# Hybrid RWKV-7 and attention block: decay taken onto the keys, group norm and rates moved along the tile

## The chip, the core and the metric

The kernel runs on one core of a Trainium2 chip. The metric is the device time of one execution in microseconds; times given for a kernel are medians of several runs on the chip. The core's engines run apart from each other and are tied by semaphores: PE (TensorE, matmuls), DVE (VectorE), ACT (ScalarE), POOL (GpSimd) and SP (SyncE, which issues most of the DMAs). Each engine takes its instructions strictly in the order in which they were issued to it.

## What is computed

One encoder block on 512 tokens of width 2048: an input projection with 86 strips of 128 columns, a bidirectional RWKV-7 branch (16 heads of 64, two directions), a grouped-query attention branch, two branch projections merged by gates, an output projection, a residual and a final norm. The part that the change touches is the RWKV recurrence and the group norm behind it:

```python
def _wkv_step(S, inp):
    w, kk, b, k, v, r = inp
    sa = jnp.einsum('dbhvk,dbhk->dbhv', S, -kk)
    S = S * w[..., None, :] + sa[..., None] * b[..., None, :] + v[..., :, None] * k[..., None, :]
    o = jnp.einsum('dbhvk,dbhk->dbhv', S, r)
    return S, o
...
    wkv = outs[0] + jnp.flip(outs[1], axis=1)
    mu = jnp.mean(wkv, axis=-1, keepdims=True)
    var = jnp.mean(jnp.square(wkv - mu), axis=-1, keepdims=True)
    gn = (wkv - mu) * lax.rsqrt(var + GN_EPS)
    gn = gn * _heads(gn_w.astype(f32)) + _heads(gn_b.astype(f32))
    coef = jnp.sum(rh[None] * k_eff * _heads(r_k.astype(f32)), axis=-1, keepdims=True).sum(0)
    out = gn + coef * vh
```

## The kernel before

The recurrence is done in chunks of 64 tokens (`NC` = 8 of them), for eight tiles of two heads each, counted here from 0 to 7. A tile passes through these steps:

- `stage_a` (L481 on), the **rates**: a 1 MB load of `la`, then `la` is mapped (L504), the sums of squares `pss` (L498) are normalised over POOL (L261) and DVE (L503) and brought back by the transposes `prb` (L508); decays are summed by a scan for each direction (L517), turned round (L522), and ACT takes exponentials (L530 to L532). POOL and DVE multiply them into the scaled keys `BK` (L538), two halves of 128 rows for each of two directions and two sources, eight instructions in all, and into `PC`, the decay of a whole chunk (L533).
- `tile_task` first forms `AL` (L556, L559), then the **chunk-local products** `lr` (L571), two chunks at a time, in four pairs with dense matmuls between them. Each pair fills two PSUM tiles; they are masked out of PSUM by four DVE instructions (L574, L575, L577, L578) and copied by two on ACT (L573, L576). All `lr` tiles come from one pool of three buffers, tag `g`.
- the **inverse**: 32x32 triangular systems, solved on DVE by 30 steps of two instructions each (L607, L608) between transposes (L592, L595, L611, L616); it ends with copies into `XX` (L622, L625). Meanwhile PE transposes `BK` (`tb`, L633).
- two small products `pq` and `px` (L645, L653), whose results ACT copies to `LQ` (L649) and `XP` (L657), complete the inverse.
- the **chain**: for each of eight chunks PE does `pa` (L678), `pu` (L693) and `px2` (L700, shown by the trace as px of L700), ACT copies between them, and DVE forms the next state `SV` (L706) from `px2` and `sd`, the old state times `PC`, which POOL has made (L689).
- `stage_e`, the **group norm** (L722 to L730 on DVE, with a POOL power at L261), then transposes `pg` (L736), ACT copies, two DVE instructions with weights, bias and gate (L742, L743), and a store by POOL.

Beside these stand the **dense matmuls** `acc` (L291), three of 128x512 for each of 16 row blocks of a strip; their weights come by SP, and each block of 12 matmuls needs one ACT cast `wh` (L264) and one DVE difference `wl` (L265). PE's order is written out by a planner, `Weave`: tasks yield a cost and a delay in planned ns, and while no task is due it puts a dense matmul, each counted with `UNIT` = 217 ns. So a delay of a task is a number of dense matmuls: `subwait` = 50000 between the last `tb` and `pq`, `c1`, `c2`, `c3` inside the chain, 2300 between pairs of `lr`. What the RWKV part does not use of the dense matmuls fills the attention part behind it. The orders on DVE, ACT, POOL and SP are set by the tile framework's scheduler, not by hand.

Of the kernel before, what the change touches and what calls it, by code (L numbers as in the profile page):

```python
# [8 lines left out]
F32 = mybir.dt.float32  # L9
F32R = mybir.dt.float32r  # L10
AF = mybir.ActivationFunctionType
ALU = mybir.AluOpType
AX = mybir.AxisListType
# [3 lines left out]
T = 512  # L17
D = 2048
NKT = 16
C = 64  # L20
NC = T // C
NT = 8
# [78 lines left out]
class Weave:  # L101
# [3 lines left out]

    UNIT = 217
    LAG = 100
# [105 lines left out]

OPT = dict(manual=True, tls=True, sub="dve", subwait=50000, fwait=6000, gn=15000, u1=0, u2=0, c1=700, c2=700, c3=1150, fly=3, scale='pool', prb=4, low=1300, warm=24, rwt='tile', every=2, auto=1, man=1)

# [9 lines left out]
def emit_all(nc, tc, A, out, dbg):  # L225
    ve, ac, po, pe, sp = nc.vector, nc.scalar, nc.gpsimd, nc.tensor, nc.sync
# [4 lines left out]
    def tap(name, ap):  # L231
        if dbg is not None and name in dbg:
            sp.dma_start(out=dbg[name], in_=ap)
# [79 lines left out]
    def temp(nm, dt=F32):  # L313
        return rw.tile([128, T], dt, name=nm, tag="e", bufs=4)
# [105 lines left out]
    def g_tile(nm):  # L420
        return pr_.tile([128, T], F32, tag="g", name=nm, bufs=3)
# [56 lines left out]

    fact = {}

    def stage_a(i):  # L481
# [21 lines left out]
        ve.tensor_copy(rb, rs[:, 8:16].rearrange("p (t h) -> p t h", h=2).unsqueeze(3).to_broadcast([128, 4, 2, C]))  # L503
        ve.tensor_scalar(out=la, in0=la, scalar1=0.5, scalar2=0.5, op0=ALU.mult, op1=ALU.add)  # L504
        yield 250, 4500, None
        prb = g_tile("prb")
        for tt in range(4):
            pe.transpose(prb[:, tt * 128:(tt + 1) * 128], rb[:, tt].rearrange("p h c -> p (h c)"), ident)  # L508
        ve.tensor_tensor(out=kk, in0=kk, in1=prb, op=ALU.mult)
        ks = rw.tile([128, T], F32, name="ks", bufs=2)  # L510
        dirs = []
# [31 lines left out]
        W.flag(f"A{i}", 6000)  # L543
        yield 428, 0, None

    def tile_task(i):
# [16 lines left out]
        for c in range(0, NC, 2):  # L563
            two = slice(c, c + 2)

            lr = [g_tile("lr").rearrange("p (d c t) -> p d c t", d=2, c=2) for _ in range(2)]
            for d in range(2):
                for j in range(2):
                    for eo in range(2):
                        h0 = 64 * eo  # L570
                        pe.matmul(lr[eo][:, d, j, :], lhsT=BK[h0:h0 + 64, d, c + j, :], rhs=AL[h0:h0 + 64, d, c + j, eo, :], start=True, stop=True)  # L571
            m2 = lambda rows, eo, c0_, c1_: mk[rows, :, eo, c0_:c1_].unsqueeze(2).to_broadcast([64, 2, 2, c1_ - c0_])
            ac.copy(LB[lo_, :, two, :], lr[0][lo_, :, :, 0:C])  # L573
            ve.tensor_tensor(out=AL[hi_, :, two, 0, :], in0=lr[0][hi_], in1=m2(hi_, 0, 0, 128), op=ALU.mult)  # L574
            ve.tensor_tensor(out=L2[lo_, :, two, 0, C:128], in0=lr[0][lo_, :, :, C:128], in1=m2(lo_, 0, C, 128), op=ALU.mult)  # L575
            ac.copy(LB[hi_, :, two, :], lr[1][hi_, :, :, C:128])  # L576
            ve.tensor_tensor(out=AL[lo_, :, two, 1, :], in0=lr[1][lo_], in1=m2(lo_, 1, 0, 128), op=ALU.mult)  # L577
            ve.tensor_tensor(out=L2[hi_, :, two, 1, 0:C], in0=lr[1][hi_, :, :, 0:C], in1=m2(hi_, 1, 0, C), op=ALU.mult)  # L578
            yield 900, 2300, None
        pv = g_tile("pv")  # L580
# [42 lines left out]
        for q in range(4):  # L623
            rows = slice(q * 32, q * 32 + 32)
            ve.tensor_copy(XB[rows], XT[1 - q % 2][rows, 1 - q % 2])  # L625
            for d in range(2):
                ac.copy(XP[rows, d, :, q * 32:(q + 1) * 32], XT[d][rows, d])

        for d in range(2):
            for g in range(2):  # L630
                tb = g_tile("tb").rearrange("p (c h t) -> p c h t", c=4, h=2)
                for j in range(4):
                    pe.transpose(tb[:, j].rearrange("p h t -> p (h t)"), BK[:, d, 4 * g + j, :], ident)  # L633
                ac.copy(L2b[:, d, 4 * g:4 * g + 4, 0:4:3, :], tb)
                yield 428, 700, None
# [26 lines left out]
        for n in range(NC):  # L662
# [20 lines left out]
            ac.copy(O[0:64, 0, both, :], pa[0:64, :, 1, :])  # L683
            sd = rw.tile([128, 2, 2, C], F32, name="sd", bufs=2)
            if n < NC - 1:
                for d in range(2):
                    for eo in range(2):
                        h = slice(64 * eo, 64 * eo + 64)
                        po.tensor_scalar(out=sd[h, d, eo, :], in0=SV[h, d, eo, 0, :], scalar1=PC[h, d, cc[d]:cc[d] + 1], scalar2=0.0, op0=ALU.mult, op1=ALU.add)  # L689
            yield 450, OPT['c1'], None  # L690
            pu = c_tile("pu").rearrange("p (d x) -> p d x", d=8)
# [9 lines left out]
            if n < NC - 1:  # L701
                SN = rw.tile([128, 2, 2, 2, C], F32, name="SV", bufs=2)
                for d in range(2):
                    for eo in range(2):
                        h = slice(64 * eo, 64 * eo + 64)
                        ve.scalar_tensor_tensor(out=SN[h, d, eo, 0, :], in0=px2[h, d, eo, :], scalar=PC[h, d, cc[d]:cc[d] + 1], in1=sd[h, d, eo, :], op0=ALU.mult, op1=ALU.add)  # L706
                SV = SN
# [4 lines left out]
        ve.tensor_tensor(out=O[:, 0], in0=O[:, 0], in1=O[:, 1], op=ALU.add)  # L712
        ow = ch(temp("ow"))
        ve.tensor_tensor(out=ow, in0=O[:, 0, 0:NC, :], in1=O[:, 0, NC:2 * NC, :], op=ALU.add)
        W.flag(f"D{i}")
        W.add(2, stage_e(i, ow, ks))
        yield 450, 0, None

    def stage_e(i, ow, ks):

        s8 = rw.tile([128, 32], F32, name="s8")
        ve.tensor_reduce(out=s8[:, 0:8], in_=ow, axis=AX.X, op=ALU.add)  # L722
        ve.tensor_scalar(out=s8[:, 8:16], in0=s8[:, 0:8], scalar1=-1.0 / C, scalar2=None, op0=ALU.mult)
# [6 lines left out]
        ve.tensor_tensor(out=ow, in0=ow, in1=s8[:, 24:32].unsqueeze(2).to_broadcast([128, NC, C]), op=ALU.mult)  # L730
        gc = temp("gc")
        yield 0, OPT['gn'], None
        for g in range(2):
            pg = g_tile("pg").rearrange("p (c e t) -> p c e t", c=4, e=2)
            for j in range(4):
                pe.transpose(pg[0:64, j].rearrange("p e t -> p (e t)"), ow[:, 4 * g + j, :], ident)  # L736
            for eo, h0 in ((1, 0), (0, 64)):
                ac.copy(ch(gc)[h0:h0 + 64, 4 * g:4 * g + 4, :], pg[0:64, :, eo, :])
            yield 428, 0, None
        sz = rw.tile([128, T], F32, name="sz", tag="sz")  # L740
        sp.dma_start(out=sz, in_=fsp[i])
        ve.scalar_tensor_tensor(out=gc, in0=gc, scalar=pc(P_GW + i), in1=ks, op0=ALU.mult, op1=ALU.add)  # L742
        ve.scalar_tensor_tensor(out=gc, in0=gc, scalar=pc(P_GB + i), in1=sz, op0=ALU.add, op1=ALU.mult)  # L743
        po.dma_start(out=osp[i], in_=gc)
        tap(f"og{i}", gc)

    W.flag("ad", 4500)
# [344 lines left out]
```

## Time and profile before

| | us |
|---|---|
| time, median of 3 runs | 1793.4 (1791.13 to 1795.57) |
| profiled execution, its own time | 1792.16 |
| its span, first to last instruction | 1789.9 |
| PE busy | 1717.1 (96%) |
| DVE busy | 1221.1 (68%) |
| ACT busy | 812.6 (45%) |
| POOL busy | 554.0 (31%) |
| mean granted share of the TensorE clock | 0.985 |

The profile is one execution. The input norm and the first two strips run to about 80 us, the RWKV tiles from there to about 1260, attention to about 1520, and the rest are branch and output projections. A matmul's end in the trace is modelled, so PE's busy share says little; what counts is how far apart the starts are, and where a row names a wait.

### The profile page before, as it was taken

Reading aid. Unit: us, or ns where it says so; the run is one execution under the profiler, and the core shown is the slowest. Engines: PE = TensorE matmul, PEld = TensorE weight load, DVE = VectorE, ACT = ScalarE, POOL = GpSimd, SP = SyncE. Lnnn points to the kernel's source line nnn. Section 1 sums busy time; section 2 is a strip of 40 time slices with the busy share of each in tenths; the row PEclk is TensorE's granted clock in tenths of the full one; section 3 lists DMA queues with packets and bytes.
Section 4 is the critical chain, followed back from the end, with each engine's and each line's share of the span. In section 5 each row is a group of like instructions: output and inputs, shape, how many; then the busy total and the mean of one; then the engine's idle time right before and its main releaser. Section 6 shows DMA issues by size and latency. Waiting matters only on the chain. (4 is left out here: it accounts for less than half of the span.)

```text
span 1789.9 us, 26075 instructions
## 1 busy us (share of the span) xinstructions
PE 1717.1 (96%) x8972; PEld 1431.3 (80%) x8972; DVE 1221.1 (68%) x2360; ACT 812.6 (45%) x1827; POOL 554.0 (31%) x824
## 2 busy tenths in 40 slices
PE   6999999999999999999999999999989998999997
PEld 6877887887887887887887888888768886788876
DVE  6577859759959948967957957923788887443342
ACT  5544354354354444344344344344566666232231
POOL 3131062053153143053053043022555554331110
PEclk9999999999999999999999999999999999999999
DMA  6564323423323322423323322433443320435452
GB/s 219 167 201 122 106 63 111 108 60 98 103 77 104 104 63 92 111 74 100 106 77 95 105 67 82 116 89 108 149 149 104 99 92 26 143 108 154 130 171 106
DMA packets 96851, 194.87 MB, mean 109 GB/s; under 512 B 11088, under 2 KB 11344, under 8 KB 95312
## 3 DMA queue, kind: packets, MB, share of 16 engines
q1 hardware_dynamic: 77616, 152.18, 29.7%
q10 hardware_dynamic: 15264, 28.46, 4.4%
q0 software_dynamic: 3840, 12.59, 2.4%
q8 instruction: 71, 1.16, 0.3%
q14 instruction: 60, 0.49, 0.1%
HBM read 162.77 MB, written 30.41 MB: 108 GB/s over the span
## 5 line engine op out<-in xcount | busy, mean ns | idle before, releaser
L291 PE MATMUL acc<-hh,wl 128*128 128x512 f32 (+1 forms) x1388 | 552.1, 398 | 5.1 <-DVE wl L265 5.1
L291 PE MATMUL acc<-hh,wh 128*128 128x512 f32 (+1 forms) x1388 | 554.2, 399 | 0.6 <-ACT wh L264 0.6
L291 PE MATMUL acc<-hl,wh 128*128 128x512 f32 (+1 forms) x1388 | 551.3, 397 | 2.8 <-DVE hl L386 2.2
L265 DVE TENSOR_TENSOR wl<-raw,wh 128x512 fp32r<-128x512 f32 x445 | 331.9, 748 | 278.7 <-ACT wh L264 268.3
L264 ACT CAST wh<-raw 128x512 fp32r<-128x512 f32 x472 | 292.3, 620 | 499.9 <-PE acc L291 348.3
L291 PEld LDWEIGHTS acc<-hh,wl 128*128 128x128 f32 x1388 | 263.2, 190 | 57.5 <-DVE wl L265 8.2
L291 PEld LDWEIGHTS acc<-hl,wh 128*128 128x128 f32 x1388 | 263.4, 190 | 53.1 <-DVE hl L386 4.2
L291 PEld LDWEIGHTS acc<-hh,wh 128*128 128x128 f32 x1388 | 263.4, 190 | 51.5 <-ACT wh L264 1.7
L673 POOL TENSOR_SCALAR SV<-VT 64x128 f32<-64x128 f32 x256 | 82.2, 321 | 214.3 <-PE px L700 110.1
L706 DVE SCALAR_TENSOR_TENSOR SV<-px,PC,sd 64x64 f32<-64x64 f32 x224 | 63.5, 283 | 79.6 <-PE px L700 73.3
L689 POOL TENSOR_SCALAR sd<-SV,PC 64x64 f32<-64x64 f32 x224 | 89.5, 400 | 17.4
L291 PE MATMUL acc<-oq,wh 128*128 128x512 f32 x256 | 84.1, 400 | 4.0 <-ACT oq L946 4.0
L607 DVE TENSOR_TENSOR tm<-B 128x30 f32<-128x30 f32 (+14 forms) x240 | 82.3, 343 | 6.1
L608 DVE TENSOR_TENSOR B<-B,tm 128x30 f32<-128x30 f32 (+14 forms) x240 | 81.1, 338 | 6.0
L527 POOL TENSOR_TENSOR ks<-ks,k 128x512 f32<-128x512 f32 x8 | 15.2, 1901 | 223.4 <-ACT wh L264 84.0
L1023 PE MATMUL of<-wl,mh 128*128 128x512 f32 x192 | 75.0, 391 | 1.8 <-DVE wl L265 1.8
L678 PEld LDWEIGHTS pa<-SV,AL 128*128 128x128 f32 x512 | 67.3, 191 | 10.2 <-POOL SV L673 2.3
L1024 PE MATMUL of<-wh,ml 128*128 128x512 f32 x192 | 74.7, 389 | 0.0
L700 PEld LDWEIGHTS px<-SV,L 128*128 128x128 f32 x512 | 67.9, 193 | 7.3 <-ACT SV L694 1.8
L678 PE MATMUL pa<-SV,AL 128*128 128x64 f32 x512 | 67.2, 271 | 3.3 <-DVE SV L706 3.3
L1022 PE MATMUL of<-wh,mh 128*128 128x512 f32 x192 | 66.1, 389 | 0.0
L700 PE MATMUL px<-SV,L 128*128 128x64 f32 x512 | 65.6, 271 | 0.0
(688 smaller groups left out, 2879.4 us busy)
## 6 DMA issues: line engine op xcount, KB each, us to landing
raw<-in_w_in_dram SPq DMA_DIRECT2D x344, 256.0 KB, 3.1
raw<-in_wo_dram SPq DMA_DIRECT2D x64, 256.0 KB, 2.8
fsp<-tg ACTq DMA_DIRECT2D x60, 256.0 KB, 2.5
tsp<-la ACTq DMA_DIRECT2D x32, 256.0 KB, 3.4
la<-tsp SPq DMA_DIRECT2D x8, 1024.0 KB, 5.0
raw<-in_wbr_dram SPq DMA_DIRECT2D x32, 256.0 KB, 3.1
tgm<-fsp POOLq DMA_DIRECT2D x32, 256.0 KB, 3.5
raw<-in_wba_dram SPq DMA_DIRECT2D x32, 256.0 KB, 2.9
```

Of the source, the lines that this page charges most:

```text
L264: ac.copy(dst_hi, src)
L265: (eng or ve).tensor_tensor(out=dst_lo, in0=src, in1=f(dst_hi), op=ALU.subtract)
L291: pe.matmul(acc[:, tok], lhsT=w[1 if u == 2 else 0][:, j, :], rhs=(xl if u == 1 else xh)[:, kt, tok], start=(kt == 0 and u == 0 and tok.st ...
L607: se.tensor_tensor(out=tv, in0=B[:, 0:s, s:s + 1].to_broadcast([128, s, n]), in1=B[:, s:s + 1, s + 1:32].to_broadcast([128, s, n]), op=ALU ...
L608: se.tensor_tensor(out=B[:, 0:s, s + 1:32], in0=B[:, 0:s, s + 1:32], in1=tv, op=ALU.add)
L673: po.tensor_scalar(out=SV[v0:v0 + 64, d, eo], in0=src.unsqueeze(1).to_broadcast([64, 2, C]), scalar1=1.0, scalar2=0.0, op0=ALU.mult, op1=A ...
L678: pe.matmul(pa[:, d, eo, :], lhsT=AL[:, d, cc[d], eo, :], rhs=SV[:, d, eo, 0, :], start=True, stop=True)
L689: po.tensor_scalar(out=sd[h, d, eo, :], in0=SV[h, d, eo, 0, :], scalar1=PC[h, d, cc[d]:cc[d] + 1], scalar2=0.0, op0=ALU.mult, op1=ALU.add)
L700: pe.matmul(px2[:, d, eo, :], lhsT=L2[:, d, cc[d], eo, :], rhs=SV[:, d, eo, 1, :], start=True, stop=True)
L1022: pe.matmul(acc, lhsT=mh[:, dt, tok(tt)], rhs=w[0], start=(dt == 0), stop=False)
L1023: pe.matmul(acc, lhsT=mh[:, dt, tok(tt)], rhs=w[1], start=False, stop=False)
L1024: pe.matmul(acc, lhsT=ml[:, dt, tok(tt)], rhs=w[0], start=False, stop=(dt == NKT - 1))
```

## The change

- The state's decay moves onto the keys: after a pair's `lr` products, ACT scales the four `BK` pieces of the pair in place by `PC` (16 instructions of 128x128 a tile). `tb`, which transposes `BK`, then carries the factor into the state's update, so that the next state is the old state times `PC` plus `px2`. POOL's `sd` goes (28 instructions a tile, 224 in all); the four DVE instructions of a step stay four, with `SV` and `px2` as their tensors instead of `px2` and `sd`.
- The two `lr` tiles of a pair come from two pools (tags `g` and `c`, three buffers each); pairs stand two by two on PE: `lr` of pairs 0 and 1 together, 23 dense matmuls, pairs 2 and 3, 14 dense matmuls, `pv`. Before, 11 stood behind each pair (7 and the block of `pg` behind the third). Half of the `tb` tiles come from tag `c` as well.
- The group norm of a tile may begin on DVE only behind the last mask of the next tile's `lr`; its `pg` stands on PE 27 dense matmuls behind `pcf`, inside the inverse.
- The mapping of `la` for the next tile (and with it what follows from it) may begin only behind the last copy of the inverse.
- `UNIT` is 227, `subwait` 51000, and the first step of the chain has 1600 more planned ns ahead of `pu` (11 dense matmuls instead of 4). Between the last `lr` of a tile and its `pq` PE has 248 to 251 dense matmuls (before 255 to 258), and 64 dense matmuls more than before are left for attention; no matmul is added or removed.

```diff
-    UNIT = 217
+    UNIT = 227
...
-OPT = dict(manual=True, tls=True, sub="dve", subwait=50000, fwait=6000, gn=15000, u1=0, u2=0, c1=700, c2=700, c3=1150, fly=3, scale='pool', prb=4, low=1300, warm=24, rwt='tile', every=2, auto=1, man=1)
+OPT = dict(manual=True, tls=True, sub="dve", subwait=51000, fwait=6000, gn=15000, u1=0, u2=0, c1=700, c2=700, c3=1150, fly=3, scale='pool', prb=4, low=1300, warm=24, rwt='tile', every=2, auto=1, man=1)
...
+    def behind(what, i):
+        return tc.issue_after(what[i].ins) if i in what else nullcontext()
...
-        ve.tensor_scalar(out=la, in0=la, scalar1=0.5, scalar2=0.5, op0=ALU.mult, op1=ALU.add)
+        with behind(inv, i - 1):
+            ve.tensor_scalar(out=la, in0=la, scalar1=0.5, scalar2=0.5, op0=ALU.mult, op1=ALU.add)
...
-            lr = [g_tile("lr").rearrange("p (d c t) -> p d c t", d=2, c=2) for _ in range(2)]
+            lr = [t_("lr").rearrange("p (d c t) -> p d c t", d=2, c=2) for t_ in (g_tile, c_tile)]
...
-            ve.tensor_tensor(out=L2[hi_, :, two, 1, 0:C], in0=lr[1][hi_, :, :, 0:C], in1=m2(hi_, 1, 0, C), op=ALU.mult)
-            yield 900, 2300, None
+            last[i] = ve.tensor_tensor(out=L2[hi_, :, two, 1, 0:C], in0=lr[1][hi_, :, :, 0:C], in1=m2(hi_, 1, 0, C), op=ALU.mult)
+            for d in range(2):
+                for j in range(2):
+                    ac.activation(BK[:, d, c + j, :], BK[:, d, c + j, :], AF.Copy, scale=PC[:, d, c + j:c + j + 1])
+            if c == 2:
+                yield 1800, 5000, None
+        W.flag(f"R{i}")
+        yield 1800, 3000, None
...
-                tb = g_tile("tb").rearrange("p (c h t) -> p c h t", c=4, h=2)
+                tb = (g_tile if g else c_tile)("tb").rearrange("p (c h t) -> p c h t", c=4, h=2)
...
-            sd = rw.tile([128, 2, 2, C], F32, name="sd", bufs=2)
-            if n < NC - 1:
-                for d in range(2):
-                    for eo in range(2):
-                        h = slice(64 * eo, 64 * eo + 64)
-                        po.tensor_scalar(out=sd[h, d, eo, :], in0=SV[h, d, eo, 0, :], scalar1=PC[h, d, cc[d]:cc[d] + 1], scalar2=0.0, op0=ALU.mult, op1=ALU.add)
-            yield 450, OPT['c1'], None
+            yield 450, OPT['c1'] + (1600 if n == 0 else 0), None
...
-                        ve.scalar_tensor_tensor(out=SN[h, d, eo, 0, :], in0=px2[h, d, eo, :], scalar=PC[h, d, cc[d]:cc[d] + 1], in1=sd[h, d, eo, :], op0=ALU.mult, op1=ALU.add)
+                        ve.scalar_tensor_tensor(out=SN[h, d, eo, 0, :], in0=SV[h, d, eo, 0, :], scalar=PC[h, d, cc[d]:cc[d] + 1], in1=px2[h, d, eo, :], op0=ALU.mult, op1=ALU.add)
...
     def stage_e(i, ow, ks):
 
+        if i < NT - 1:
+            yield 0, 0, f"R{i + 1}"
         s8 = rw.tile([128, 32], F32, name="s8")
-        ve.tensor_reduce(out=s8[:, 0:8], in_=ow, axis=AX.X, op=ALU.add)
+        with behind(last, i + 1):
+            ve.tensor_reduce(out=s8[:, 0:8], in_=ow, axis=AX.X, op=ALU.add)
```

What this does to the order on DVE shows first between the chain of one tile and the inverse of the next. Before, from the sum of the outputs (L714) into the third pair of masks; `s` is the group norm's small tile, `cs` a scan of the rates:

```order
L714 TENSOR_TENSOR ow<-O 128x512
L504 TENSOR_SCALAR la<-la 128x2048
L722 TENSOR_REDUCE s_5145<-ow 128x8
L517 SCALAR_TENSOR_TENSOR cs_5897<-con,la 128x512
L265 TENSOR_TENSOR wl<-raw,wh 128x512
L475 SCALAR_TENSOR_TENSOR tg<-tg,acc 128x512
L723 TENSOR_SCALAR s_5145<-s_5145 128x8
L522 TENSOR_TENSOR cs_5897<-cs_5897 128x512
L724 TENSOR_TENSOR ow<-ow,s_5145 128x512
L574 TENSOR_TENSOR AL<-lr,con 64x2x2x128
```

Now, from the same sum (L725 of the changed kernel):

```order
L725 TENSOR_TENSOR ow<-O 128x512
L265 TENSOR_TENSOR wl<-raw,wh 128x512 x2
L582 TENSOR_TENSOR AL<-lr,con 64x2x2x128
L583 TENSOR_TENSOR L_533<-lr,con 64x2x2x64
L585 TENSOR_TENSOR AL<-lr,con 64x2x2x128
L586 TENSOR_TENSOR L_533<-lr,con 64x2x2x64
```

The masks stand directly behind the sum; the group norm's eight instructions stand now behind the last mask, before and inside the inverse, and `la`, the first scan and its turning have left this place.

Second, DVE behind the inverse, up to the first new state of the chain. Before (tile 4), where `cs` is the one scan that is left, `ke` the second direction's keys:

```order
L625 COPY XX<-RR 32x256 x2
L265 TENSOR_TENSOR wl<-raw,wh 128x512
L305 SCALAR_TENSOR_TENSOR v<-acc,par,v 128x511
L306 SCALAR_TENSOR_TENSOR v<-acc,par,v 128x511
L265 TENSOR_TENSOR wl<-raw,wh 128x512
L500 TENSOR_SCALAR rs<-pss 128x8
```

Now (tile 5), the same stretch; L505 is the old L500:

```order
L640 COPY XX<-RR 32x256 x2
L510 TENSOR_SCALAR la<-la 128x2048
L265 TENSOR_TENSOR wl<-raw,wh 128x512
L534 TENSOR_SCALAR ks<-la,par,der 128x512
L525 SCALAR_TENSOR_TENSOR cs_8339<-con,la 128x512
L265 TENSOR_TENSOR wl<-raw,wh 128x512
L305 SCALAR_TENSOR_TENSOR v<-acc,par,v 128x511
L530 TENSOR_TENSOR cs_8339<-cs_8339 128x512
L306 SCALAR_TENSOR_TENSOR v<-acc,par,v 128x511
L265 TENSOR_TENSOR wl<-raw,wh 128x512
L505 TENSOR_SCALAR rs<-pss 128x8
```

Four instructions of the rates and one `wl` more stand ahead of `rs`. From `rs` on the order is as before: in tiles 1, 2, 5 and 6 all eight `BK` instructions stand ahead of the first new state (L715), as in tile 4 before; in tile 3 six of them, in tiles 0 and 4 four. Tile 7 has no next tile and no rates.

Third, ACT around `pq` of tile 5 now; `e` and `cs` are exponentials of the scan that DVE makes behind `rs`:

```order
L264 CAST wh<-raw 128x512 x2
L538 ACTIVATE e_8330<-cs_8324 128x512
L539 ACTIVATE cs_8324<-cs_8324 128x512
L540 ACTIVATE la<-la 128x512
L664 COPY LQ<-pq 32x8x32 x4
L264 CAST wh<-raw 128x512
```

The copies of `pq` stand behind those exponentials, as they did before (L530 to L532 ahead of L649); what they wait for is the scan, which the second place has moved.

## Rows read from the trace of the kernel before

**Rows 1.** Page, part 1: busy time of each engine, share of the span, instructions.
```profile
PE 1717.1 (96%) x8972; PEld 1431.3 (80%) x8972; DVE 1221.1 (68%) x2360; ACT 812.6 (45%) x1827; POOL 554.0 (31%) x824
```

**Rows 2.** Windows, lr stretches of tiles 1 to 6: window, length, PE, PEld, DVE, ACT, POOL, clock.
```profile
core 0: us, PE busy (x) PEld busy (x) DVE busy (x) ACT busy (x) POOL busy (x), PEclk, DMA share, GB/s
...
689.00:709.60 20.60, 16.88 (x106) 13.35 (x106) 15.93 (x27) 8.42 (x20) 4.75 (x4) 0.83 0.23 64
...
sum 107.30, PE 91.24 PEld 71.97 DVE 90.57 ACT 53.33 POOL 28.43; mean PE 15.21 PEld 11.99 DVE 15.09 ACT 8.89 POOL 4.74
```

**Rows 3.** Windows: lr of tile 7, end of attention, dense alone, behind a wait.
```profile
1101.50:1115.40 13.90, 13.85 (x106) 11.06 (x106) 11.79 (x21) 8.02 (x18) 2.95 (x2) 1.00 0.33 95
1490.00:1524.00 34.00, 26.59 (x151) 20.59 (x150) 24.83 (x57) 19.99 (x43) 15.69 (x20) 0.92 0.13 41
1600.00:1640.00 40.00, 40.00 (x178) 33.01 (x177) 11.49 (x17) 10.10 (x17) 2.78 (x2) 1.00 0.43 128
690.00:706.00 16.00, 12.33 (x65) 9.52 (x63) 13.10 (x22) 5.63 (x12) 3.45 (x3) 0.79 0.28 75
```

**Rows 4.** Timeline of PE, tile 4: start, length, row, idle before it and releaser.
```profile
697.01 2.04 PE L571 MATMUL lr<-AL,BK 64*128 64x128 f32 x14 [3.67 <-DVE s L728]
707.29 1.50 PE L571 MATMUL lr<-AL,BK 64*128 64x128 f32 x16
...
771.73 1.86 PE L645 MATMUL pq<-XX,LQ 128*128 128x32 f32 x16
...
783.11 1.00 PE L678 MATMUL pa<-SV,AL 128*128 128x64 f32 x8
```

**Rows 5.** Groups of PE and of POOL: busy, mean ns of one, idle before, releaser.
```profile
L693 PE MATMUL pu<-a0s,XP 128*128 128x64 f32 x256 | 37.7, 271 | 5.8 <-ACT a0s L681 5.8
L633 PE MATMUL tb<-con,BK 128*128 128x128 f32 x128 | 19.4, 274 | 4.4 <-ACT VT L584 3.6 <-DVE L L575 0.7
L689 POOL TENSOR_SCALAR sd<-SV,PC 64x64 f32<-64x64 f32 x224 | 89.5, 400 | 17.4
L680 ACT COPY a0s<-pa 64x128 f32<-64x128 f32 x64 | 16.6, 259 | 13.3 <-PE pa L678 12.8
```

**Rows 6.** Timeline of DVE, tile 3: masks of pair 1, gates, inverse's first and last.
```profile
558.67 0.69 DVE L574 TENSOR_TENSOR AL<-lr,con 64x512 f32<-64x512 f32 x1
...
560.86 0.69 DVE L265 TENSOR_TENSOR wl<-raw,wh 128x512 fp32r<-128x512 f32 x1
...
565.63 1.22 DVE L742 SCALAR_TENSOR_TENSOR gc<-gc,par,ks 128x512 f32<-128x512 f32 x1 [0.56 <-ACT gc L738]
566.89 0.75 DVE L743 SCALAR_TENSOR_TENSOR gc<-gc,par,sz 128x512 f32<-128x512 f32 x1
567.55 0.54 DVE L526 TENSOR_SCALAR ks<-la,par,der 128x512 f32<-128x512 f32 x1
568.11 0.69 DVE L574 TENSOR_TENSOR AL<-lr,con 64x512 f32<-64x512 f32 x1
...
617.28 0.59 DVE L625 COPY XX<-RR 32x256 f32<-32x256 f32 x2
```

**Rows 7.** Timeline of DVE, tile 4: inverse's end, rates, first new state.
```profile
760.64 0.59 DVE L625 COPY XX<-RR 32x256 f32<-32x256 f32 x2
...
764.98 0.17 DVE L500 TENSOR_SCALAR rs<-pss 128x8 f32<-128x8 f32 x1 [0.46 <-PE pss L498]
...
782.24 1.23 DVE L706 SCALAR_TENSOR_TENSOR SV<-px,PC,sd 64x64 f32<-64x64 f32 x4
```

**Rows 8.** Timeline of DVE, rates ahead of tile 3's masks, at their place before.
```profile
549.52 1.22 DVE L504 TENSOR_SCALAR la<-la 128x2048 f32<-128x2048 f32 x1
...
551.25 1.22 DVE L517 TENSOR_TENSOR_SCAN cs<-con,la 128x512 f32<-128x512 f32 x1
```

**Rows 9.** Timeline of POOL, tile 4: the turned decays of the first scan.
```profile
692.25 1.59 POOL L523 TENSOR_TENSOR la<-cs,la 128x512 f32<-128x512 f32 x1 [8.19 <-DVE cs L522]
```

**Rows 10.** Timeline of DVE, tile 4: the row beside it.
```profile
692.63 1.76 DVE L265 TENSOR_TENSOR wl<-raw,wh 128x512 fp32r<-128x512 f32 x1
```

## What I expect of the change, and why

> **What bounds the kernel now.** I read the page's busy times first. PE is busy for 96% of the span, DVE for 68, ACT for 45, POOL for 31 [rows 1]. No matmul is added or removed, so PE's work stays, and the time moves by what PE loses: waits, and stretches at the lower clock. I went to those next. While nothing disturbs it, a dense matmul takes 40.00 / 178 = 0.225 us [rows 3], and PE's order is fixed. A wait is therefore lost in full unless dense matmuls stand in its place.
>
> The windows of the `lr` stretches show the largest loss of one kind. Each of tiles 1 to 7 has 106 matmuls between its first and last `lr`. Tile 7 needs 13.9 us for them [rows 3], tiles 1 to 6 together 107.3 [rows 2]. Six times 13.9 is 83.4, so 23.9 us are lost there. The timeline of tile 4 shows how: an `lr` stands 3.67 us for `s` of L728 [rows 4], which is the group norm of the tile before: DVE does its instructions ahead of the masks, all three PSUM buffers are full, and PE waits. Behind this wait the granted clock falls to 0.79 on the mean of 16 us [rows 3], which is part of the time at 1.2 GHz instead of 2.4; 0.21 x 16 = 3.4 us go there, about as much as the wait itself, and they lie inside the 23.9.
>
> The other end of DVE's load is the chain's head. In tile 4 the last copy of the inverse ends at 760.64 + 0.59 = 761.23, and the first new state starts at 782.24 [rows 7], 21.0 us later; `pa` of the second step, which needs that state, is at 783.11 [rows 4]. So the state comes just in time. PE's own side is `pq` at 771.73, and 10.5 us of its own instructions to the same point. Whatever delays DVE here meets PE with no cover left.
>
> **What the change removes.** First, the 23.9 us. The masks now stand directly behind the sum of the outputs; `lr` has two pools with three buffers each, and pairs stand in twos with 23 dense matmuls (5.2 us) between. I take all of it as gone. Second, `tb`'s waits, 4.4 us, of which 3.6 are for ACT's copies at L584 [rows 5]: with half the tiles in the other pool, gone as well. Third, `pu`'s waits in front of the first steps, 5.8 us [rows 5]; 7 more dense matmuls stand there (1.6 us for each tile), and I count them as gone here and put what DVE does to this place into the sum below. Together 34.1. Fourth, the end of attention: between 1490 and 1524 PE is busy for 26.59 of 34.00 us [rows 3], so 7.4 are idle; 64 more dense matmuls go to attention, 18 of them into its last eight units. 18 x 0.225 = 4.0 is what they could fill, nothing the other bound; I take 2. That is 36.
>
> Priced at nothing: POOL's `sd`, 89.5 us [rows 5], because POOL is busy for 31% and PE's state waits for `px2` anyway; the form of `SV`, four instructions on the same sizes; the 16 scalings on ACT, each about as long as the copy of half the partitions and equal length, 0.26 us [rows 5], so 4.2 us a tile. They stand between `lr` and `tb`, where 14 dense matmuls (3.2 us) and the last pair cover them, and ACT is busy for 45%. If that cover fails, up to 4.2 us a tile wait at `tb`: that is a rival below.
>
> **What it adds.** It doesn't add work to DVE, it moves work into the stretch between `lr` and the chain's head, which was full.
>
> Inverse: before, tile 4 took 761.23 - 708.79 (707.29 + 1.50) = 52.4 us from the last `lr` to the last copy [rows 4, 7]. The group norm's eight instructions now come in behind the last mask: four of 0.69 (the size of a mask), two of 0.17, 1.22 and 0.75 [rows 6, 7], 5.1 us. By the order one `wl` and one or two instructions of its size leave the same stretch, 1.4 to 2.1. That gives 52.4 + 3.0 = 55.4 us. Tile 3 agrees: its last mask to its last copy is 617.87 - 568.11 = 49.8 us [rows 6], with gates of the tile before (L742, L743) standing ahead of it, which now stand in it.
>
> From the last copy to the first state: 21.0, less the wait of 0.46 for `pss` [rows 7], is 20.5. Now `la` (1.22) and the first scan (1.22) [rows 8], `ks` (0.54), the turning and one more `wl` (0.69 each) [rows 6] stand ahead of `rs`: 4.4 us, together 24.9. POOL turns too: two POOL instructions of 1.59 [rows 9] now run beside this stretch. Beside the row of 1.59 a `wl` took 1.76 instead of 0.69 [rows 6, 9, 10], so 1.07 were lost. The bounds for both are nothing (no DVE row falls on them) and 2 x 1.59. I take nothing, because DVE also has short idle pieces between these rows that the 4.4 can fill, and keep the other end for a rival. In this order the first state starts 55.4 + 24.9 = 80.3 us behind the last `lr`.
>
> The Trainium skill says in "SBUF — State Buffer", section "SBUF: two separate sides", that VectorE and GpSimd share a port pair as an exclusive lock: a GpSimd instruction that starts first holds off a VectorE instruction with two SBUF inputs for its whole length. The trace agrees: the POOL row ends at 693.84, 0.69 behind that is 694.53, and the `wl` ended at 694.39 [rows 9, 10]. By this rule two such rows cost up to 3.2 us for a tile, by my term nothing.
>
> What PE allows: `pq` stood 771.73 - 708.79 = 62.9 us behind the last `lr` [rows 4]. Seven dense matmuls fewer take off 1.6, `tb`'s waits 4.4 / 8 = 0.5; `pg` now stands inside, four transposes and what goes with them, about 0.9 as an estimate from 0.274 for one of 128x128 [rows 5]. So 61.7. To the point where the state is wanted it was 10.5, and 7 dense matmuls more make 12.1; I allow 12.5, since `pa` came 0.9 behind the state's start. That is 74.2.
>
> So a full tile waits 80.3 - 74.2 = 6.1, I take 6.0 (5 to 8). Tiles 1, 2, 5 and 6 have all eight `BK` instructions ahead of the first state: 24.0. Tile 3 has six, two of 0.69 fewer: 4.6. Tiles 0 and 4 have four; there the wait is about half of a tile's for each at most, I take 3 for both. Tile 7 has no rates: none. Sum 31.6. A wait of this size can be followed by the lower clock, as in rows 3, at 0 to 3.4 us each. Part of that falls into a place where PE would wait anyway; I take 0.7 in each of five tiles, 3.5. Added: 35.
>
> The profiled execution took 1792.2 us (span 1789.9 and 2.3 around it); 1792.2 - 36 + 35 = 1791. The median of the runs is 1.2 above this execution, less than any term.
>
> **Rivals.** *The head of the chain is covered.* If the rates' instructions find DVE idle, or the scheduler's row sums are 6 us too long, the new waits don't arise and only the gain is left: 1792.2 - 36 = 1756 (1745 to 1772). For it: 96% of PE's span is work and DVE has 32% free over the whole. Against it: between the inverse and the first state DVE's rows stand nearly end to end [rows 6, 7], and tile 4 was just in time.
>
> *POOL and DVE exclude each other (slower).* The two POOL rows that were moved hold up DVE for their whole length, 2 x 1.59 = 3.2 us a tile. Full tiles then wait 9.2; with four of them, tile 3 and half a tile each for 0 and 4 that is 5.5 x 3.2 = 17.6 more: 1809 (1799 to 1820, the upper end with the clock's 3.4 in most tiles). It decides from about 1.5 us a tile on. For it: the pair of rows 9 and 10. The rule of the Trainium skill's "SBUF — State Buffer" quoted above says the same. Against it: POOL's rows meet DVE at their start only by chance.
>
> *The change doesn't do what it says.* The 16 scalings hold up ACT's copies, PSUM comes free late and half of the 23.9 at `lr` stays: 1791 + 12 = 1803. Against it: six buffers instead of three, and an ACT that is busy for 45%.
>
> **How the numbers follow.** The forecast, that the wait moves from `lr` to the chain's head and gain and loss are nearly equal, has 0.45, with 1791 and a range of its own of 1778 to 1802 (5 to 8 us for a full tile, and the clock). The covered head has 0.27, mutual exclusion 0.22, the failing change 0.06. A measurement of this kernel can tell about 0.3%, 5.4 us, from no change: 1788.0 to 1798.8 counts as the same. Below this lie nearly all of the second case and 0.17 of the first: 0.44. Above it lie the third, the fourth and 0.03 of the first: 0.31. For the same 0.25 is left. The range of 1753 to 1811 leaves out about a third of the covered head and near half of the third case, some 0.19.
>
> **What would show it.** In the profile of the changed kernel the `lr` stretches of tiles 1 to 6 should each take 14 to 15 us for their matmuls and the waits of `lr` and `tb` should be gone. In tiles 1, 2, 3, 5 and 6 PE should wait at the chain's head, for ACT's `LQ` or for `SV`, some 6 us in all before the second `pa`, with granted clocks below 0.9 behind it; tiles 4 and 7 should have little of it. The last copy of the inverse should come some 6 us ahead of `pq` instead of 10.5. Attention should take up to 64 x 0.225 = 14.4 us longer and the part before it shorter. If no wait stands at the chain's head, the first rival is right; if `lr` still waits, the last one; if DVE's rows in front of `rs` take twice their length beside POOL, the third.

## The result, and the profile after

The changed kernel takes 1819.25 us (median of 4 runs, 1816.01 to 1821.25), the kernel before 1793.08 beside it: a ratio of 1.0143 (95% interval 1.0122 to 1.0165). It is slower by 26 us, where I expected 1791, and it lies above the range.

The busy times, and the group of `pa`, from the page of the changed kernel (busy us, mean ns | idle before, releaser):

```profile
PE 1720.5 (95%) x8972; PEld 1440.1 (79%) x8972; DVE 1221.8 (67%) x2358; ACT 853.8 (47%) x1955; POOL 467.2 (26%) x602
...
L693 PE MATMUL pa<-SV,AL 128*128 128x64 f32 x512 | 69.3, 277 | 14.1 <-DVE SV L715 14.1
```

The work is that of before [rows 1]: ACT has 128 scalings more, POOL some 220 instructions fewer. What was to go has gone. The windows of the `lr` stretches of tiles 1 to 6 (window, length, busy time of each engine, granted clock), of which tile 4 and the sum:

```profile
690.20:699.70 9.50, 9.50 (x89) 8.05 (x88) 6.26 (x12) 6.62 (x19) 0.00 (x0) 1.00 0.39 113
...
sum 57.00, PE 57.00 PEld 48.33 DVE 36.80 ACT 41.87 POOL 0.00; mean PE 9.50 PEld 8.06 DVE 6.13 ACT 6.98 POOL 0.00
```

Every one of them has PE busy from end to end at full clock, where tiles 1 to 6 lost 23.9 us [rows 2, 3]. They hold 89 matmuls where there were 106, since `pg` and some of the dense matmuls no longer stand in them. The groups of `tb` and `pu` have 0.0 and 0.2 us of idle time instead of 4.4 and 5.8 [rows 5].

The loss stands at a place that the prediction doesn't name: `pcf`, the two matmuls behind `tb` that sum the bonus of the heads from `ch` and `cl`. Three of their groups in the changed kernel (one instruction each, then idle before it):

```profile
L653 PE MATMUL pcf<-cl__6516,blk 128*128 128x512 f32 x1 | 0.8, 796 | 0.7 <-POOL cl__6516 L265 0.7
...
L652 PE MATMUL pcf<-ch__6515,blk 128*128 128x512 f32 x1 | 0.8, 792 | 5.3 <-ACT ch__6515 L264 5.3
...
L652 PE MATMUL pcf<-ch__1484,blk 128*128 128x512 f32 x1 | 0.4, 395 | 0.0
```

In tile 0, which has no group norm ahead of it, there is no wait; in tiles 1 to 7 `pcf` waits 3.9 to 5.3 us for `ch` (31.1 in all) and about 0.7 for `cl` (5.0). Before, none of these waited. The timelines of tile 4 tell why. First PE (start, length, row, idle before it and releaser):

```profile
708.64 0.39 PE L291 MATMUL acc<-hh,wh 128*128 128x512 f32 x1
714.31 0.79 PE L652 MATMUL pcf<-ch__6515,blk 128*128 128x512 f32 x1 [5.28 <-ACT ch__6515 L264]
715.78 0.80 PE L653 MATMUL pcf<-cl__6516,blk 128*128 128x512 f32 x1 [0.68 <-POOL cl__6516 L265]
716.37 0.63 PE L291 MATMUL acc<-hl,wh 128*128 128x512 f32 x1
```

Then ACT in the same stretch:

```profile
710.28 0.58 ACT L649 COPY L<-tb 128x512 f32<-128x512 f32 x1
713.12 0.63 ACT L740 ACTIVATE os__6477<-ow 128x512 f32<-128x512 f32 x1 [2.26 <-DVE ow L738]
713.65 0.60 ACT L264 CAST ch__6515<-ks 128x512 fp32r<-128x512 f32 x1
```

And DVE, from the last mask on:

```profile
703.96 0.43 DVE L586 TENSOR_TENSOR L<-lr,con 64x256 f32<-64x256 f32 x1
704.42 0.69 DVE L736 TENSOR_REDUCE s<-ow 128x8 f32<-128x512 f32 x1
...
710.54 0.17 DVE L737 TENSOR_SCALAR s<-s 128x8 f32<-128x8 f32 x1
710.61 1.90 DVE L610 STREAM_TRANSPOSE B<-FT 128x1024 f32<-128x1024 f32 x1
712.43 0.65 DVE L738 TENSOR_TENSOR ow<-ow,s 128x512 f32<-128x512 f32 x1
```

`ch` is a cast of `ks`, which had been ready since the rates (L549, done at 641.2). But on ACT it stands directly behind `os`, the square of the group norm. That waits for `ow` of L738, and L738 now stands on DVE behind the last mask and, between other parts of the inverse, behind a transpose of 1.90 us. So a chain that PE didn't need until `pg` reaches PE through ACT's queue at `pcf`. Behind such a wait the clock falls; the window from 714.3 on has it at 0.50, which is 1.2 GHz:

```profile
714.30:720.40 6.10, 5.41 (x12) 3.98 (x13) 4.86 (x15) 0.62 (x1) 2.97 (x2) 0.50 0.30 86
```

Over the span the mean granted clock is 0.973, before 0.985.

### The profile page after: what moved, and what is told of

It is laid out like the page before. It is cut to its first block, busy times and chain, and to the rows that moved or that the text cites. A ratio compares the mean times of both kernels' runs of the same rounds, so it can differ in the third digit from the quotient of the medians.

```text
span 1814.2 us, 26169 instructions
## 1 busy us (share of the span) xinstructions
PE 1720.5 (95%) x8972; PEld 1440.1 (79%) x8972; DVE 1221.8 (67%) x2358; ACT 853.8 (47%) x1955; POOL 467.2 (26%) x602
## 5 line engine op out<-in xcount | busy, mean ns | idle before, releaser
L291 PE MATMUL acc<-hh,wl 128*128 128x512 f32 (+1 forms) x1388 | 558.0, 402 | 5.2 <-DVE wl L265 5.1
L291 PE MATMUL acc<-hl,wh 128*128 128x512 f32 (+1 forms) x1388 | 557.2, 401 | 2.8 <-DVE hl L386 2.3
L291 PEld LDWEIGHTS acc<-hh,wl 128*128 128x128 f32 x1388 | 267.1, 192 | 58.6 <-DVE wl L265 8.5
L291 PEld LDWEIGHTS acc<-hl,wh 128*128 128x128 f32 x1388 | 267.3, 193 | 54.7 <-DVE hl L386 4.3
L291 PEld LDWEIGHTS acc<-hh,wh 128*128 128x128 f32 x1388 | 267.2, 192 | 50.2 <-ACT wh L264 0.2
L688 POOL TENSOR_SCALAR SV<-VT 64x128 f32<-64x128 f32 x256 | 87.9, 343 | 410.5 <-PE acc L291 169.3
L715 DVE SCALAR_TENSOR_TENSOR SV<-SV,PC,px 64x64 f32<-64x64 f32 x224 | 62.7, 280 | 78.8 <-PE px L709 72.9
L717 ACT COPY O<-px 64x128 f32<-64x128 f32 x64 | 16.7, 260 | 104.9 <-DVE SV L715 84.7
```

The lines of the kernel that those rows point to most:

```text
L291: pe.matmul(acc[:, tok], lhsT=w[1 if u == 2 else 0][:, j, :], rhs=(xl if u == 1 else xh)[:, kt, tok], start=(kt == 0 and u == 0 and tok.st ...
L688: po.tensor_scalar(out=SV[v0:v0 + 64, d, eo], in0=src.unsqueeze(1).to_broadcast([64, 2, C]), scalar1=1.0, scalar2=0.0, op0=ALU.mult, op1=A ...
L715: ve.scalar_tensor_tensor(out=SN[h, d, eo, 0, :], in0=SV[h, d, eo, 0, :], scalar=PC[h, d, cc[d]:cc[d] + 1], in1=px2[h, d, eo, :], op0=ALU. ...
```

## The experiments

Two theories stood against each other. Theory Q: the loss is where PE meets the late group norm through a queue. Theory H: it is at the head of the chain, as predicted, DVE having too much between the last `lr` and the first new state. The kernel before took 1790.4 to 1791.2 us beside these runs, and 1793.1 beside the changed kernel. A plain difference between a run and the changed kernel therefore holds some 2 us that are not the edit's; where it matters, a second figure compares how far each lies above its own kernel before. Each edit also lets the scheduler order the other engines anew. In tile 4, four `BK` instructions stand on DVE ahead of the first new state in the changed kernel, none with `ch` ahead of the square, and eight with the group norm back. So a run tells what an edit is worth together with the order that came with it.

**`ch` ahead of the square.** The whole edit:

```diff
+        ch_, cl_ = temp("ch_", F32R), temp("cl_", F32R)
+        split(ch_, cl_, ks, po)
         W.flag(f"R{i}")
         yield 1800, 3000, None
...
-        ch_, cl_ = temp("ch_", F32R), temp("cl_", F32R)
-        split(ch_, cl_, ks, po)
```

> The changed kernel, but the cast `ch` and the difference `cl`, which feed `pcf`, are issued ahead of the flag that lets the group norm start, so that on ACT `ch` stands ahead of the group norm's square `os` and no longer behind it. No work is added or taken away, and PE's order stays. Theory Q (a wait in ACT's queue): in the changed kernel seven `pcf` wait for `ch` (31.1 us together) and `cl` (5.0), and 6.8 to 10.2 us at granted clock 0.50 follow each, at least 7 x 3.4 = 24 us; that is all of the loss, so about 1819 - 60 = 1759 (1750 to 1770), with no new wait elsewhere. Theory H (head of the chain, as predicted): DVE's rows between the last lr and the first state are the bound; PE then only reaches `pq` about 8 us earlier in each tile and waits there for `XX`, `LQ` or `SV`; 1785 to 1805, waits of 5 to 8 us a tile at pq, px and pa.

1806.77 us, 1.0088 of before (1.0071 to 1.0105): 12.5 less than the changed kernel (10.1 against the kernels before). `pcf` waits no more, and what follows it does. PE in tile 4:

```profile
706.92 0.39 PE L652 MATMUL pcf<-ch__6473,blk 128*128 128x512 f32 x1
707.14 0.40 PE L653 MATMUL pcf<-cl__6474,blk 128*128 128x512 f32 x1
...
716.95 0.82 PE L751 MATMUL pg<-con,ow 128*64 128x128 f32 x3 [3.29 <-DVE ow L744]
```

Of 36 us of waits, 14.6 are back at `pg`, the group norm's own next place on PE, and 5.9 at `prb`, which had waited 0.6. Neither theory holds alone: the queue was real, and much of the waiting came back behind it.

**`pg` later too.** `gn=25000` instead of 15000, on top of the last edit.

> The kernel with `ch` ahead of the group norm's square (1807), and the group norm's transposes `pg` 44 dense matmuls (10 us) later (its delay 25000 instead of 15000), so that PE waits for the group norm neither at pcf nor at pg (17 us there before, and the clock). Theory Q (the loss is where PE meets the late group norm): 1775 to 1790. Theory H (DVE is the bound between the last lr and the first state; each wait that is removed returns behind it): 1798 to 1808, with pq, px, pa and prb waiting longer than the 36 us that they sum to there.

1790.97 us, 1.0007 of before (0.9997 to 1.0017): another 15.8 less (15.5 against the kernels before). With `pcf` and `pg` clear of it, these groups of the recurrence still wait longest:

```profile
L693 PE MATMUL pa<-SV,AL 128*128 128x64 f32 x512 | 69.9, 280 | 12.5 <-DVE SV L715 12.5
...
L709 PE MATMUL px<-SV,L 128*128 128x64 f32 x512 | 66.4, 273 | 5.9 <-ACT SV L703 5.9
...
L668 PE MATMUL px<-XX,LQ 128*128 128x32 f32 x128 | 17.2, 291 | 6.1 <-ACT LQ L664 6.1
...
L514 PE MATMUL prb<-con,rb 128*128 128x128 f32 x32 | 5.3, 294 | 6.1 <-DVE rb L508 6.1
```

Together 30.6 us, all of it around `pq` and in the first steps of the chain. Apart from `prb`, which the prediction didn't name, these are the places where it had put the waits of the changed kernel, and the time is the one that it forecast. The 28.3 us from here to the changed kernel, 12.5 and 15.8 (25.6 against the kernels before), are what it left out.

**The group norm at its old place.** Its two conditions are taken out of the changed kernel, all else stays:

```diff
-        if i < NT - 1:
-            yield 0, 0, f"R{i + 1}"
...
-        with behind(last, i + 1):
-            ve.tensor_reduce(out=s8[:, 0:8], in_=ow, axis=AX.X, op=ALU.add)
+        ve.tensor_reduce(out=s8[:, 0:8], in_=ow, axis=AX.X, op=ALU.add)
```

> The changed kernel with one part undone: the group norm starts as soon as the outputs are summed, as before (neither the flag nor the order behind the last mask). Rates behind the inverse, scaled keys, two pools and the numbers of the planner stay. Theory Q: `os` then stands far ahead of `ch` on ACT and is ready early, so the waits of `pcf` go (60 us with the clock), and waits of `lr` come back in part, since the group norm stands ahead of the masks again, 0 to 24 us as before the change, less with six buffers: 1760 to 1785. Theory H: DVE has 5 us less between the last lr and the first state; what is left of waits at the head is 0 to 3 us a tile: also some 1770 to 1790, but with the waits at pq, px and pa as the largest.

1773.95 us, 0.9904 of before (0.9887 to 0.9921). That is 45 us less than the changed kernel (43 against the kernels before), and faster than both. The rows that wait in it:

```profile
L693 PE MATMUL pa<-SV,AL 128*128 128x64 f32 x512 | 69.2, 278 | 11.6 <-DVE SV L715 11.6
...
L668 PE MATMUL px<-XX,LQ 128*128 128x32 f32 x128 | 15.4, 274 | 4.7 <-ACT LQ L664 4.7
...
L748 PE MATMUL pg<-con,ow 128*64 128x128 f32 x64 | 9.8, 281 | 7.6 <-DVE L L583 6.8 <-ACT BK L590 0.8
...
L514 PE MATMUL prb<-con,rb 128*128 128x128 f32 x32 | 5.3, 294 | 4.3 <-DVE rb L508 4.3
```

No `lr` waits, although the group norm stands ahead of the masks again. On PE `pg` now comes directly behind the last `lr`, and there it waits 7.6 us, most of it for a mask; in the kernel before it stood between the third and the fourth pair and didn't wait. Both theories allowed this time, so it alone doesn't decide between them. It does say which part of the change loses.

**The rates at their old place**, the group norm staying behind the masks: the condition on `la` is taken out.

```diff
-        with behind(inv, i - 1):
-            ve.tensor_scalar(out=la, in0=la, scalar1=0.5, scalar2=0.5, op0=ALU.mult, op1=ALU.add)
+        ve.tensor_scalar(out=la, in0=la, scalar1=0.5, scalar2=0.5, op0=ALU.mult, op1=ALU.add)
```

> The changed kernel with the other part undone: the mapping of `la` and what follows from it are no longer held behind the last copy of the inverse. The group norm stays behind the masks. Theory Q: the waits at `pcf` stay as they are (36 us and the clock), only the waits of pa for `SV` (14.1 us) and of px for `LQ` (3.3) get shorter: 1800 to 1815. Theory H: the head of the chain is where the loss is, so undoing what was put there gives most of the 26 us back: 1785 to 1798.

1825.55 us, 1.0192 of before (1.0177 to 1.0208): slower than the changed kernel by 6 (9 against the kernels before). Both expectations missed, and theory H missed in the direction too: undoing what it blamed makes the kernel slower. The longest single wait of this kernel is again at `pcf`, longer than the 4.9 us that the same tile waits in the changed kernel:

```profile
L651 PE MATMUL pcf<-ch__5255,blk 128*128 128x512 f32 x1 | 0.8, 797 | 8.1 <-ACT ch__5255 L264 8.1
```

The rates' instructions stand ahead of the masks again, the masks end later, and the whole chain of the group norm with them: in tile 3 the last mask ends 9.3 us behind the last `lr` instead of 5.9, and the square 16.9 instead of 13.7.

**Both at their old places**, that is, both edits above in one kernel.

> The changed kernel with both moves undone: neither the group norm nor the rates are held behind anything; scaled keys, two pools, pairs by twos, the planner's numbers stay. Theory G (the group norm's new place is the whole loss, the rates' place is harmless or good): about the time of the run with the group norm alone undone, 1774, or a few us above it, 1772 to 1782, because the rates' instructions stand ahead of the masks again. Theory R (the rates' place costs at the chain's head): waits of pa, px and prb (11.6, 3 to 5 and 5 us in the run with the group norm undone) go and nothing comes: 1750 to 1765.

1784.60 us, 0.9972 of before (0.9960 to 0.9983). So with the group norm at its old place the rates' move is worth 10.7 us (1784.6 against 1774.0). `lr` waits only 0.1 us here too, so the two pools and the new order of the pairs are enough for it. What the rates' move saves shows at `pg` behind the last `lr`, 19.2 us here against 7.6 there:

```profile
L747 PE MATMUL pg<-con,ow 128*64 128x128 f32 x64 | 11.7, 317 | 19.2 <-DVE L L582 8.3 <-ACT BK L589 4.9 <-ACT LB L580 3.4
```

**Only the keys scaled**, in the kernel before: the 16 scalings, no `sd`, the new form of the state.

```diff
-            sd = rw.tile([128, 2, 2, C], F32, name="sd", bufs=2)
...
+            for d in range(2):
+                for j in range(2):
+                    ac.activation(BK[:, d, c + j, :], BK[:, d, c + j, :], AF.Copy, scale=PC[:, d, c + j:c + j + 1])
```

> The kernel before with the first part of the change alone: keys scaled by `PC` on ACT, 16 scalings a tile, no `sd` on POOL, state = old state times `PC` plus `px2`. Order of the group norm, rates, pools and all numbers of the planner as before. If the scaling costs nothing and gives nothing, as the sum had it: 1788 to 1798. If the 4.2 us a tile on ACT hold up the copies out of `lr` and through them PSUM (the rival of a change that doesn't do what it says): more waits of lr and tb, 1800 to 1825.

1789.27 us, 0.9996 of before (0.9985 to 1.0007): nothing either way, as the sum had it, for 89.5 us of POOL's work removed and 128 instructions on ACT added.

**Filling the head of the chain.** In the kernel with the group norm at its old place PE still waits there. More dense matmuls between `tb` and `pq` cost nothing if they stand where PE would wait: `subwait=53500`, and then `56000`, instead of 51000.

> The kernel with the group norm undone (1774), and `subwait` 53500 instead of 51000: 11 more dense matmuls (2.5 us) between the last tb and `pq` of each tile, taken from attention. If the waits left at the head of the chain (pa for `SV` 11.6 us, px for `LQ` some 3 to 5, prb some 5, and seven stretches of 3.4 to 6.8 us at half clock) are DVE being late, the filling takes their place and the clock stays up: 1774 - (7 x 2.5, less what tiles without a wait lose nothing by) = 1755 to 1766. If attention needs the 88 dense matmuls as much, nothing is won: 1772 to 1778.

> As the run before it, with `subwait` 56000: 22 more dense matmuls (5 us) a tile, 176 in all. Lateness of DVE: the head of the chain is free of waits and the rest of the gain is small, 1750 to 1765; attention needs them: 1770 to 1785, with new waits of sc, pT and po.

1765.94 us (0.9864 of before, 0.9847 to 0.9882) and 1777.87 us (0.9929, 0.9907 to 0.9951). The first is as expected, 8 us less. The second loses it again, and not only in attention, where the waits grow by a few us. In tile 3 PE waits 6.10 us for `LQ`, which ACT copies late. PE of this kernel:

```profile
632.17 2.13 PE L668 MATMUL px<-XX,LQ 128*128 128x32 f32 x9 [6.10 <-ACT LQ L664]
```

And its ACT:

```profile
622.75 0.60 ACT L264 CAST wh<-raw 128x512 fp32r<-128x512 f32 x1
630.26 0.33 ACTq L476 DMA_DIRECT2D fsp<-tg  x1
630.63 1.49 ACT L664 COPY LQ<-pq 32x256 f32<-32x256 f32 x4 [7.27 <-DVE tg L475]
```

Here the copies of `pq` stand behind the store of a gate strip, which waits for `tg`, and `tg` stands on DVE behind keys. It is the same kind of fault, in another place: what PE waits for stands in a queue behind something that is late for reasons of its own.

**`prb` later.** In the run with 53500 the largest wait left in the RWKV part is this one:

```profile
L514 PE MATMUL prb<-con,rb 128*128 128x128 f32 x32 | 5.4, 294 | 12.5 <-DVE rb L508 12.5
```

`rb` stands on DVE behind the rates that the change put behind the inverse. The delay ahead of `prb` becomes 8000 instead of 4500:

> The run with the group norm undone and `subwait` 53500 (1766), and the transposes `prb` 15 dense matmuls (3.5 us) later behind `pss`: its delay 8000 instead of 4500. There `prb` waited 13.6 us for `rb`, which stands on DVE behind the rates' instructions since these are behind the inverse. If that wait is lateness alone: 1766 - 13 = 1753, less still if the four stretches of 3.4 us at half clock go too (1748 to 1758). If the keys that follow `prb` come later in turn and the first new state behind them on DVE: no gain, 1764 to 1770, with longer waits of pa for `SV`.

1762.46 us, 0.9841 of before (0.9827 to 0.9854), the fastest of all. `prb` waits 0.0 us now, but only 3.5 us of 12.5 are won, between the two expectations, and the intervals of the two runs overlap. The kernel's waits for `LQ` and `SV` grow from 0.0 and 5.3 us.

```profile
L693 PE MATMUL pa<-SV,AL 128*128 128x64 f32 x512 | 67.8, 273 | 6.7 <-DVE SV L715 6.7
...
L668 PE MATMUL px<-XX,LQ 128*128 128x32 f32 x128 | 15.5, 275 | 3.7 <-ACT LQ L664 3.7
```

**The group norm behind the masks with every cover.** The same two numbers, with `ch` ahead of the square and `pg` late:

> The changed kernel with its group norm behind the masks, `ch` ahead of the square and `pg` late (1791), and the two fillings of the run beside it: `subwait` 53500 and `prb` 3.5 us later. Theory H says that what is left of the loss against the run beside it is the group norm's 5 us on DVE between the last lr and the first state: 7 tiles at 2 to 3 us, so 12 to 25 us above the run beside it, 1768 to 1780. If the place of the group norm costs nothing once no queue meets it late: equal to it within 5 us.

1791.27 us, 0.9996 of before (0.9986 to 1.0007): 29 us above the run beside it, more than theory H allowed, and no faster than without the two numbers. Its waits:

```profile
L693 PE MATMUL pa<-SV,AL 128*128 128x64 f32 x512 | 71.0, 283 | 5.5 <-DVE SV L715 5.5
...
L896 PE MATMUL sc<-KH,Q 128*128 128x512 f32 x64 | 28.5, 445 | 11.9 <-ACT pr L902 10.2 <-DVE Q L872 1.4
...
L668 PE MATMUL px<-XX,LQ 128*128 128x32 f32 x128 | 20.5, 323 | 12.0 <-ACT LQ L664 12.0
```

From the last `lr` to the last copy of the inverse, tiles 1 to 6 take 54.5 us on the mean here and 52.1 in the run beside it (starts of the last `lr`, ends of the last copy). Six times 2.4 is 14 us; `LQ` (12.0 against 3.7) and the first `sc` of attention (11.9 against 6.9) show about 13 us of it. The other half of the 29 I can't put to one place. Up to the last `px` of the chain this kernel takes 20.7 us longer (1220.0 against 1199.3), behind it 9. The mean granted clock is 0.975 against 0.983, which is 14.8 us of the spans (0.025 x 1789.3 less 0.017 x 1759.7). Part of the low clock lies under waits that are counted already, and no run separates the two.

## Why the prediction was wrong

**The step that failed** is the one on the inverse: "The group norm's eight instructions now come in behind the last mask". It counts DVE's eight and prices them by their lengths. But the moved piece also has an instruction on ACT, the square `os`. It moved with them, to the place directly ahead of `ch`, and the prediction says nothing of that place; the order of ACT that it reads is that around `pq`. Of the other queue the prediction says "`pg` now stands inside, four transposes and what goes with them, about 0.9", which prices their work and not whether `ow` is ready. (They are eight transposes, but start within 0.8 us in tile 4, so the price of the work holds.) In the prediction's own terms the sum for PE has no wait in it: `pq` was to stand 61.7 us behind the last `lr`, and in tiles 1 to 7 of the changed kernel it stands 68.1 to 70.5 behind. These two queue positions together cost 28.3 us (12.5 for `ch`, 15.8 for `pg`, each by its own run), or 25.6 against the kernels before. The forecast is short by 28.2. That the two figures meet so closely is partly luck, since other terms of the sum are off and cancel, as shown below.

**Removed.** Right at every place: `lr` 23.9, `tb` 4.4, `pu` 5.8 have gone. Attention and what follows it were to take up to 14.4 us longer: from the last `px` of the chain (starting at 1224.08 before and 1238.57 after) to the end of the span it is 565.8 and 575.6, so 9.8 longer. If nothing else moved there, the other 4.6 filled idle places, where the prediction took 2.

**Priced at nothing.** Right: the scaled keys measure 0.9996. The 16 scalings cost ACT more than the sum had, 42.8 us in all or 5.4 a tile instead of 4.2, and the kernel with the scaling alone doesn't show it.

**The head of the chain.** Right in place once the two queues were cleared, and near in the total: 30.6 us of waits, 24.5 without `prb`, against the 31.6 of the sum. In tile 6 of that kernel, where all eight `BK` instructions stand ahead of the first state (a full tile), the four marks are these, from the answers for one line each (last column of times: first and last start):

```profile
L579 PE MATMUL lr<-AL,BK x64: 272/272/373, 954.8 to 964.1; 64*128 64x128 f32 x64
...
L660 PE MATMUL pq<-XX,LQ x16: 195/276/276, 1025.7 to 1027.3; 128*128 128x32 f32 x16
...
L640 DVE COPY XX<-RR x4: 281/284/291, 1016.3 to 1017.8; 32x256 f32<-32x256 f32 x4
...
L715 DVE SCALAR_TENSOR_TENSOR SV<-SV,PC,px x12: 273/280/289, 1044.9 to 1058.8; 64x64 f32<-64x64 f32 x12
```

The last `lr` ends at 964.3. The inverse ends 53.8 us behind it (forecast 55.4), `pq` starts 61.4 behind it (61.7), and the first state 26.8 us behind the inverse (24.9), so 80.6 behind the last `lr` (80.3). The other full tiles, 1, 2 and 5, have 79.5 to 80.4. Tile by tile the waits are not those of the sum. The full tiles wait 2.4 to 5.2 us each, `prb` included, where it has 6, and tiles 0 and 4 wait about 4 and 6, where it has 3 for both. In tile 4 the stretch on DVE isn't full. DVE stands idle for 10.0 of the 22.1 us between the inverse and the first state, the longest piece for `pss`, which stands on PE behind `pa` there:

```profile
760.98 0.17 DVE L505 TENSOR_SCALAR rs<-pss 128x8 f32<-128x8 f32 x1 [3.96 <-PE pss L503]
```

The keys then come behind the first state, and the wait of 4.04 us is for the second one, which stands behind most of them. The clock behind such waits was sized too small: this kernel runs at 0.976 of full clock on the mean against 0.985, which is 16 us of its span (0.024 x 1787.6 less 0.015 x 1789.9), where I took 3.5. Part of the low clock lies under waits, and no run here separates the two. That its time is 1791 as well therefore owes something to terms that cancel.

**Which move loses.** I put the rates at 4.4 us a tile and the group norm at 3.0. By the runs the rates' move wins 10.7 us with the group norm at its old place, and 6 to 9 with the group norm at the new one. The group norm's move loses 43 to 45 us as it stands, and 29 with every cover that I tried. Its old place costs little, the 7.6 us of waits at `pg`: once the rates have left it, DVE has slack there, with 6.13 of 9.50 us busy in the `lr` stretches of the changed kernel.

**The rivals.** The head of the chain covered (1756) did not come by itself, but 1762 was reached with the group norm back, eleven more dense matmuls and `prb` later. POOL and DVE shutting each other out gave a time nearer to the measured one (1809) for a reason that the runs don't bear out: 45 us go with the group norm's place, while the two POOL rows stay where the change put them. Its sign does show in part. In tiles 1 to 6 of the changed kernel one `wl` ahead of `rs` takes 1.71 to 1.72 us instead of 0.69 beside a POOL row, in tiles 5 and 6 a second one 1.34 and 1.78:

```profile
761.30 2.06 POOL L535 TENSOR_TENSOR ks<-ks,k 128x512 f32<-128x512 f32 x1 [31.22 <-DVE ks L534]
...
762.20 1.72 DVE L265 TENSOR_TENSOR wl<-raw,wh 128x512 fp32r<-128x512 f32 x1
```

That is 1.0 to 2.1 us a tile, between the nothing of the sum and the 3.2 of the rival. What it costs the kernel has not been measured alone. (The rival's own sum counts 5.5 tiles where its list makes 6, so 1810.) The failing change (1803) is out, since `lr` waits for nothing.

## What to carry to other kernels

When a group of instructions is moved on one engine, list its members on every engine, and for each the next two or three instructions in that queue: what matters is who stands behind it and who waits for those, not how long it takes. Here an instruction of 0.6 us, issued one place ahead of a cast, held PE up for 31 us in seven tiles, while the sum priced DVE's work alone. A wait that is taken away shows what stands behind it, so price a removal by a run: 36 us of waits at `pcf` were worth 10 to 12.5.

## What the runs showed of the chip that I had not expected

The wait of 5.3 us at `pcf` is followed by 6.1 us at a granted clock of 0.50, in which 12 matmuls were done. At full clock these take 12 x 0.225 = 2.7 us, and 0.68 is the wait for `cl`, so the first wait costs about 2.7 us more than itself. In tiles 1 to 7 the second `pcf` takes 0.79 to 0.80 us, where it takes 0.39 in tile 0, so the same happens in each of them. In the run with `pg` late two shorter waits, 1.82 us for `LQ` and 4.04 for `SV`, are each followed by such a stretch, with 0.57 and 0.51 on the mean of 8 and 7 us:

```profile
757.00:765.00 8.00, 8.00 (x35) 7.14 (x35) 2.26 (x5) 3.02 (x9) 2.10 (x2) 0.57 0.12 33
778.00:785.00 7.00, 6.80 (x24) 6.06 (x25) 2.96 (x7) 2.22 (x9) 3.13 (x5) 0.51 0.26 78
```

In the first of them PE was busy all the time, so a low clock doesn't show as idle time of any row.
